# One product in eight left out of a last quarter, norm factors moved behind sums, softmax by heads

## The chip, the cores and the metric

The kernel runs on one core of one Trainium2 chip. Its time is the device time of an execution in microseconds (us); of several runs the median is taken. One further execution was recorded by the hardware profiler, and all rows in the profile's views are of that one.

## What is computed

A trunk of two layers over 16 + 512 = 528 positions of width 1024, in float32. Each layer is a mixer, a residual, an MLP and a residual; cut to what matters here:

```python
def sq_relu_mlp(h, norm_g, w_up, w_down):
    return jnp.square(jax.nn.relu(rms_norm(h, norm_g) @ w_up)) @ w_down   # 1024 -> 4096 -> 1024

h = h + even_mixer(h, ...)             # layer 0: attention (8 heads, window 128, sinks) beside a state-space scan
h = h + sq_relu_mlp(h, mlp_norm[0], w_up[0], w_down[0])
h = h + conformer_conv_module(h, ...)  # layer 1: pointwise, gate, causal depthwise convolution with 31 taps, layer norm, pointwise
h = h + sq_relu_mlp(h, mlp_norm[1], w_up[1], w_down[1])
return h[:, 16:]
```

`rms_norm` divides each position by its root mean square. This factor is one number r per position, so relu(r x) = r relu(x), and the square carries r squared, which may be multiplied behind the down projection.

## The kernel before

**Dense products.** Activations lie transposed: features on the 128 partitions, in 8 tiles, positions along the free axis. The positions are two streams, A with 272 (the 16 meta tokens and blocks 1 and 2) and B with 256 (blocks 3 and 4); in the second layer's MLP both have 256. Weights and activations are split into a high part of a float32 type that TensorE takes in one pass and a low part (the rest). A product of two tiles is three matmuls, high x high, high x low, low x high (`products`, L456). `dense` (L468) runs over output tiles n and the k-tiles of the inner dimension; a result gathers in a PSUM bank and is handed to an evacuation thread. The weight split is made on the chip, for each stream again: `th_load` fetches a piece (tile name `wr`) of 8 k-tiles (pool `wp`) or 4 (pool `wm`), `th_cast` makes the high part `wh` on ScalarE (L280), `th_low` the low part `wl` on VectorE (L254) or GpSimd (L256).

**An MLP** (`mlp`, L1317) goes by quarters q of the 4096 inner features: 8 output tiles of the up projection, then 8 of the down projection with those as inner k-tiles, one stream at a time. A stage's name gives its kind, layer, quarter and stream: `up13B` is the up projection of layer 1, quarter 3, stream B. The up evacuation (`ev_up`) takes relu times the norm's factor `rb` on VectorE, the square and the high part `ah` on ScalarE, the low part `al` on VectorE. In quarter 0 the factor isn't known yet: there relu stands alone, and the down evacuation multiplies by the factor's square. `add_h` adds each quarter's result to the residual `h`; `fin` (L1604) adds the last one and sends it out.

**Order of the work.** `main` (L1381) goes: first projection `in` for both streams; output projection `out` of A; quarters 0 and 1 of A's first MLP, beside which attention and scan of blocks 3 and 4 run on; `out` of B; quarters 2 and 3 of A; first pointwise product `pw` of A; the four quarters of B; `pw` of B; second pointwise product of A; four quarters of A's second MLP (`up10A` to `dn13A`); second pointwise product of B; four quarters of B (`up10B` to `dn13B`). The depthwise convolutions (`th_conv`, L1484) run on VectorE beside the MLPs: stream A's beside the first MLP of B, stream B's beside the second MLP of A; layer norms (`th_ln`) follow them. `wp` takes over the attention's memory, when the last attention block and the scan's norm of B are done.

**Who sets the order on the engines.** The kernel is written as threads; a planner (`Sched`, L66) emits their operations one at a time, by a cost table. An operation can have several ways (VectorE or GpSimd); `emit` takes the one that ends first by the plan, plus a handicap that the way may carry (`bias`: 3000 ns against VectorE for low parts while the convolutions run, 0 in the last stages). Among threads the one that can start first goes, then the lower rank: evacuations 0.5, loads 0, casts 1, low parts 1 or 4, convolution 3, attention blocks 1 and 2 by `rank` 0.6, later ones 2. The plan counts a port that VectorE (with both inputs in SBUF) and GpSimd share.

**Attention** (`att(c)`, L883) for block c: for each of four head pairs the scores on TensorE (`att_a`), then on VectorE the bias and the row maximum (L907). `softmax(g)` starts when all four heads of a group have their maxima: a small operation on the maxima `am`, four exponentials on ScalarE with row sums, the sink's term `ae`, the reciprocal, scaling; then transposes (`att_b`) and the products with the values (`att_c`). `ssd_norm` (L1104) gates the scan's output with silu and normalises it for `out`, in units of blocks whose ranks `UR` gives.

## Time and profile before

| | before |
|---|---|
| time, median of 3 runs | 1241.56 us (1237.67 to 1242.43) |
| time of the profiled execution | 1237.84 us |
| its span, first to last instruction | 1236.1 us |
| granted TensorE clock, mean | 0.994 |
| busy: TensorE, VectorE, ScalarE, GpSimd | 1219.7, 861.5, 683.4, 549.5 us |
| moved from and to HBM | 190.62 MB read, 2.10 MB written |

How the views are read: PE is TensorE's matmul, PEld its weight load, DVE VectorE, ACT ScalarE, POOL GpSimd, SP the queue that issues DMAs. A row of the views by line gives source line, engine, operation, `out<-in` by tile names, shape, count, then busy time, mean duration in ns, and the idle time before these instructions with what ended it. A row of the timeline gives start, duration, engine, line, operation; in brackets the idle time before it. A row of busy time by stretch gives the stretch, its length, for PE, PEld, DVE, ACT and POOL the busy time and number of instructions, then the clock, the DMA share and GB/s. A row of the chain gives start, duration and what ran in the chain of work that ended last. Matmuls overlap, so a single one shows some 280 ns where the next one starts after less than half of it.

### The profile page before, as it was taken

The numbers are of one execution on the slowest core, as the hardware profiler recorded it, in microseconds if no ns is written. First come the engines' busy times: TensorE is split into PE (matmuls) and PEld (weight loads), VectorE is DVE, ScalarE is ACT, GpSimd is POOL, SyncE is SP. The second block draws the span as 40 slices with busy tenths as digits, with TensorE's granted clock in tenths as the row PEclk, the third lists the DMA queues.
The fourth block names the chain that finished last, engine by engine and source line by source line (L and its number), as shares of the span: only waits on it lengthen the run. The fifth ranks groups of instructions, "written<-read, shape, count | busy, mean of one in ns | idle before, by whom it ended". The sixth has DMA issues, their size and how long they took to land.

```text
span 1236.1 us, 25626 instructions
## 1 busy us (share of the span) xinstructions
PE 1219.7 (99%) x9939; PEld 1176.1 (95%) x9939; DVE 861.5 (70%) x1915; ACT 683.4 (55%) x1277; POOL 549.5 (44%) x339
## 2 busy tenths in 40 slices
PE   8999998999999999999999999999999999999998
PEld 7999887799898999999999999999999999999998
DVE  6745685787785675658989965589898626766664
ACT  6654235677475663654544568556345645644542
POOL 0112331354541111148888878888888781000000
PEclk8999999999999999999999999999999999999999
DMA  6323112344344765546555555565555566566562
GB/s 191 105 81 86 44 44 56 104 141 144 114 142 135 245 198 176 172 135 199 183 184 181 185 166 180 187 192 175 181 186 183 176 194 202 188 179 196 177 196 91
DMA packets 79961, 194.38 MB, mean 157 GB/s; under 512 B 8912, under 2 KB 16608, under 8 KB 79840
## 3 DMA queue, kind: packets, MB, share of 16 engines
q1 hardware_dynamic: 79840, 192.75, 50.2%
q8 instruction: 78, 1.28, 0.4%
q14 instruction: 43, 0.35, 0.1%
HBM read 190.62 MB, written 2.10 MB: 156 GB/s over the span
## 4 chain that ended last, share of the span: by engine, by line
PE 92%; DVE 3%; ACT 3%; issue 1%; DMA 1%; SPq 0%; DVEq 0%; ACTq 0%
PE in L308 11%; PE pw L308 9%; PE out L308 5%; PE dn00A L308 2%; PE up00A L308 2%; PE up01A L308 2%; PE up03A L308 2%; PE dn02A L308 2%; PE dn12A L308 2%; PE up03B L308 2%; PE dn13B L308 2%; PE dn12B L308 2%; PE dn11B L308 2%; PE dn10B L308 2%; PE dn11A L308 2%; PE dn03B L308 2%
## 5 line engine op out<-in xcount | busy, mean ns | idle before, releaser
L256 POOL TENSOR_TENSOR wl<-wr,wh 128x1024 fp32r<-128x1024 f32 (+1 forms) x292 | 519.2, 1798 | 432.1 <-ACT wh L280 315.3
L280 ACT CAST wh<-wr 128x512 fp32r<-128x512 f32 (+1 forms) x494 | 384.6, 801 | 287.7 <-PE in L308 35.1
L254 DVE TENSOR_TENSOR wl<-wr,wh 128x512 fp32r<-128x512 f32 (+1 forms) x202 | 189.3, 949 | 90.0 <-ACT wh L280 87.1
L261 DVE SCALAR_TENSOR_TENSOR conv<-U,vec,conv 128x256 f32<-128x256 f32 x464 | 211.3, 484 | 5.2
L308 PE MATMUL in<-xh,wh 128*128 128x272 f32 (+1 forms) x384 | 103.6, 296 | 1.4 <-ACT wh L280 1.2
L308 PE MATMUL in<-xl,wh 128*128 128x272 f32 (+1 forms) x384 | 100.8, 289 | 1.1 <-DVE xl L261 1.1
L308 PE MATMUL pw<-nh,wh 128*128 128x256 f32 (+1 forms) x320 | 80.3, 285 | 0.0
L308 PE MATMUL pw<-nl,wh 128*128 128x256 f32 (+1 forms) x320 | 80.1, 284 | 0.0
L308 PEld LDWEIGHTS in<-xh,wh 128*128 128x128 f32 x384 | 73.3, 191 | 6.9 <-issue 3.2
L308 PEld LDWEIGHTS in<-xl,wh 128*128 128x128 f32 x384 | 73.3, 191 | 2.3 <-DVE xl L261 2.0
L308 PE MATMUL in<-xh,wl 128*128 128x272 f32 (+1 forms) x384 | 66.9, 291 | 0.0
L308 PEld LDWEIGHTS pw<-nl,wh 128*128 128x128 f32 x320 | 60.3, 189 | 0.0
L308 PEld LDWEIGHTS pw<-nh,wh 128*128 128x128 f32 x320 | 60.2, 188 | 0.1
L308 PEld LDWEIGHTS in<-xh,wl 128*128 128x128 f32 x384 | 55.0, 192 | 1.6 <-issue 0.9
L308 PE MATMUL pw<-nh,wl 128*128 128x256 f32 (+1 forms) x320 | 48.4, 284 | 0.0
L276 ACT ACT_TABLE_LOAD x30 | 38.5, 1283 | 9.0 <-DMA hin<-in_h 4.6
L308 PEld LDWEIGHTS pw<-nh,wl 128*128 128x128 f32 x320 | 42.8, 188 | 0.0
L308 PE MATMUL out<-xh,wh 128*128 128x272 f32 (+1 forms) x128 | 33.0, 288 | 0.2 <-ACT acc L276 0.2
L308 PE MATMUL out<-xl,wh 128*128 128x272 f32 (+1 forms) x128 | 32.6, 285 | 0.0
L254 DVE TENSOR_TENSOR pw<-pw,rb 128x272 f32<-128x272 f32 (+1 forms) x32 | 14.1, 440 | 24.9 <-PE pw L308 24.9
L308 PEld LDWEIGHTS out<-xh,wh 128*128 128x128 f32 x128 | 24.1, 188 | 1.4 <-issue 0.8
L308 PEld LDWEIGHTS out<-xl,wh 128*128 128x128 f32 x128 | 24.1, 188 | 0.0
(597 smaller groups left out, 3642.5 us busy)
## 6 DMA issues: line engine op xcount, KB each, us to landing
wr<-in_w_up SPq DMA_DIRECT2D x84, 512.0 KB, 3.7
wr<-in_w_dn SPq DMA_DIRECT2D x84, 512.0 KB, 4.0
wr<-in_w_up SPq DMA_DIRECT2D x88, 256.0 KB, 4.3
wr<-in_w_dn SPq DMA_DIRECT2D x88, 256.0 KB, 4.3
wr<-in_w_p SPq DMA_DIRECT2D x36, 512.0 KB, 3.9
wr<-in_w_in SPq DMA_DIRECT2D x48, 256.0 KB, 2.9
wr<-in_w_out SPq DMA_DIRECT2D x36, 256.0 KB, 2.8
wr<-in_w_p SPq DMA_DIRECT2D x24, 256.0 KB, 5.2
```

Source lines behind the costliest of these rows:

```text
L254: ways = [("V", 1.04 * n + 145, lambda: nc.vector.tensor_tensor(o, a, b, op=op), sb(a) and sb(b))]
L256: ways.append(("G", 2.17 * n + 170, lambda: nc.gpsimd.tensor_tensor(o, a, b, op=op), True))
L261: lambda: nc.vector.scalar_tensor_tensor(o, a, s, b, op0=op0, op1=op1), sb(a) and sb(b))],
L276: return Op([("A", ns, lambda: nc.scalar.activation(o, a, f, **kw), False)], aps(o, accum), aps(a, scale, bias), table=TABLE.get(f, 0))
L280: return Op([("A", 0.836 * cols(o) + 192, lambda: nc.scalar.copy(o, a), False)], [o], [a])
L308: nc.tensor.matmul(o, lhsT=l, rhs=r, start=st, stop=sp)
```

## The change

**The last quarter of the second MLP** is done for both streams together (`mlp` with `last`). Its up projection runs with one set of weight pieces for both streams, output tiles in the order 0, 4, 1, 5, ... . Its down projection is a product of 2 x 2 blocks: two output tiles n and n + 1, two halves of the 8 k-tiles, two streams as two column blocks. A scheme with seven products in place of eight (Strassen's, in Winograd's form) is used for four such pairs. The weight factors of four products are sums of weight pieces, made by the new thread `th_sum` (VectorE or GpSimd, handicap half of `bias`) before they are split; the activation factors T1 to T4 are sums of squares, made and split by `sums_of`. Stream B's squares of the first four tiles aren't split themselves. `seven` issues the products M1 to M7; `ev` forms the four results and adds them to `h` in two steps each (`fin_part`), which are then sent out from `h` itself. `bias` is 600 there, and up to seven PSUM banks may be used.

**Order.** Stream A's quarters 0 to 2 are followed at once by the second pointwise product of B, then B's quarters 0 to 2, then the joint quarter 3.

**Quarters summed first.** For stream B's first MLP (four quarters) and stream A's second one (three quarters), no quarter uses the norm's factor in its up evacuation: relu is an operation of its own on ScalarE, and the down results are summed in SBUF (`tot`; the first quarter is copied there by ScalarE). The last one multiplies the sum by the factor's square and goes on to the residual. Quarter 0 of the other MLPs has its relu on ScalarE too, and so has the convolution's first tap (L1499 before).

**Softmax head by head.** Each head has a thread of its own, from its maximum to its exponential with row sum; `softmax` goes on when four heads are done.

**Planner.** `ssd_norm`'s ranks go from 1.5 to 0.5 and from 0.4 to 0.3. While an operation of rank 0.5 or lower that can use VectorE's SBUF port waits, GpSimd may not take a less urgent operation that would end after that one's start. `row_norm` uses one PSUM bank in place of two in turn.

```diff
+        rank = lambda th: th[1]() if callable(th[1]) else th[1]
+
+        urgent = min((max(th[3].dep, self.free["V"]) for th in self.threads if th[3] is not None and rank(th) <= URGENT
+                      and any(w[0] == "V" and w[3] for w in th[3].ways)), default=None)
         for th in self.threads:
             op = th[3]
             if op is None:
                 continue
-            t = min(self.start(op, w)[0] for w in op.ways)
+            ways = op.ways
+            if urgent is not None and rank(th) > URGENT:
+                ways = [w for w in ways if not (w[0] == "G" and w[3] and self.start(op, w)[1] > urgent)]
+                if not ways:
+                    continue
+            t = min(self.start(op, w)[0] for w in ways)
...
+    def expect_seven(pairs):
+
+
+        for one, two in pairs:
+            i = len(plan)
+            half = lambda j, x: (j, 4 * x)
+            plan.extend((("wp", one, 8, None), ("wp", two, 8, "raw"),
+                         ("wm", (ALU.add, half(i + 1, 0), half(i + 1, 1)), 4, "sum"),
+                         ("wm", (ALU.subtract, half(i, 0), half(i + 1, 0)), 4, "sum"),
+                         ("wm", (ALU.subtract, half(i + 2, 0), half(i, 0)), 4, "sum"),
+                         ("wm", (ALU.subtract, half(i, 1), half(i + 4, 0)), 4, "sum"),
+                         ("wm", half(i + 1, 1), 4, "half")))
+            uses.extend((4, 4, 2, 1, 2, 1, 1))
...
+    def th_sum():
+        i = 0
+        while True:
+            yield lambda: i < len(plan) or over
+            if i >= len(plan):
+                return
+            if plan[i][3] == "sum":
+                op, (a, x), (b, y) = plan[i][1]
+                yield lambda: a in raws and b in raws
+                t = yield take(wm, [128, 4, 128], F32, "raw", 4, "ws")
+                o = TT(t, raws[a][:, x:x + 4], raws[b][:, y:y + 4], op, True)
+                o.ways[0] += (bias[0] / 2,)
+                yield o
+                raws[i] = t
+                used_raw(a, b)
+            i += 1
...
+        heads_done = [set(), set()]
+
+        def head(g, i):
+            mi = m[g][:, i:i + 1]
+            yield STT(mi, mi, -1.0, nsink[:, 4 * g + i:4 * g + i + 1], ALU.mult, ALU.min)
+            yield ACT(Sx[g][:, i, :nk], Sx[g][:, i, :nk], AF.Exp, bias=mi, accum=d[g][:, i:i + 1])
+            heads_done[g].add(i)
...
+                spawn(head(g, i), rank(c, 0.6), "att")
         pm = mt.tile([128, 8, 16], F32, tag="pm", bufs=1, name=nm("pm"))
 
         def softmax(g):
-            sk = nsink[:, 4 * g:4 * g + 4]
-            yield STT(m[g], m[g], -1.0, sk, ALU.mult, ALU.min)
-            yield TT(e[g], m[g], sk, ALU.subtract)
-            for i in range(4):
-                yield ACT(Sx[g][:, i, :nk], Sx[g][:, i, :nk], AF.Exp, bias=m[g][:, i:i + 1], accum=d[g][:, i:i + 1])
+            yield lambda: len(heads_done[g]) == 4
+            yield TT(e[g], m[g], nsink[:, 4 * g:4 * g + 4], ALU.subtract)
...
-    UR = lambda u: {0: 1.5, 2: 0.4}.get(u[0], 1)
+    UR = lambda u: {0: 0.5, 2: 0.3}.get(u[0], 1)
...
+            j = n - first
             u = p[:, :w]
-            if q:
+            if late:
+                yield ACT(u, u, AF.Relu)
+            else:
                 yield after(key)
                 yield STT(u, u, 0.0, rb[s][:, :w], ALU.max, ALU.mult)
-            else:
-                yield TS(u, u, 0.0, None, ALU.max)
+            if last:
+                raw[s, j] = yield take(pool7[0], [128, 272], F32, "sq", 8)
+                r = raw[s, j][:, :w]
+                yield ACT(r, u, AF.Square)
+                drop(p)
+                sums.add((s, j))
+                if s == 0 or j >= 4:
+                    yield CP(ah[:, j, :w], r)
+                    yield TT(al[:, j, :w], r, ah[:, j, :w].bitcast(F32), ALU.subtract)
+                    up[i].add(j)
+                return
...
+            if late:
+
+                if tot is not None and late != "last":
+                    if late == "first":
+                        tot[n] = yield take(pool7[0], [128, 272], F32, "sq", 8)
+                        yield CP(tot[n][:, :w], p[:, :w])
+                    else:
+                        yield TT(tot[n][:, :w], tot[n][:, :w], p[:, :w], ALU.add)
+                    drop(p)
+                    return
+                r2 = (acc if layer or tot is None else rb)[s][:, :w]
                 yield after(key)
-                if (key, 2) not in done:
+                if (key, 1) not in done:
+                    done.add((key, 1))
+                    yield TT(r2, rb[s][:, :w], rb[s][:, :w], ALU.mult)
                     done.add((key, 2))
-                    yield TT(r2, rb[s][:, :w], rb[s][:, :w], ALU.mult)
+                yield after((key, 2))
+                if tot is not None:
+                    yield TT(p[:, :w], tot[n][:, :w], p[:, :w], ALU.add)
+                    drop(tot.pop(n))
...
+    SEVEN = (0, 4, 1, 5, 2, 6, 3, 7)
...
+    def sums_of(k, w, there, raw, up, summed):
+        yield lambda: {(0, k), (1, k)} <= there
+        x1, y1 = raw[0, k], raw[1, k]
+        yield lambda: k in up[0]
+        yield TT(x1[:, :256], y1[:, :256], x1[:, :256], ALU.subtract, True)
+        yield lambda: (1, k + 4) in there
+        y2 = raw[1, k + 4]
+        yield TT(y1[:, :256], y2[:, :256], y1[:, :256], ALU.subtract, True)
+        yield lambda: k + 4 in up[1]
+        yield TT(y2[:, :256], y2[:, :256], x1[:, :256], ALU.subtract, True)
+        if w > 256:
+            yield VCP(y2[:, 256:w], x1[:, 256:w])
+        yield lambda: k + 4 in up[0]
+        x2 = raw[0, k + 4]
+        yield TT(x2[:, :w], y2[:, :w], x2[:, :w], ALU.subtract, True)
+        for i, t in ((1, x1), (3, y1), (2, y2), (4, x2)):
+            n = w if i in (2, 4) else 256
+            hi, lo = slot(i, 0, k, n), slot(i, 1, k, n)
+            yield CP(hi, t[:, :n])
+            yield TT(lo, t[:, :n], hi.bitcast(F32), ALU.subtract, True)
+            drop(t)
+            summed[i - 1].add(k)
...
+        def product(p, hi, lo, x, first, last_, ks=range(4)):
+            xh_, xl_, when, n = ops[x]
+            for k in ks:
+                yield lambda: when(k)
+                yield MM([(p[:, :n], hi[:, k], xh_(k), first and k == 0, False),
+                          (p[:, :n], hi[:, k], xl_(k), False, False)])
+            for k in ks:
+                yield MM([(p[:, :n], lo[:, k], xh_(k), False, last_ and k == 3)])
...
+            yield CP(m1[:, :w], b[0][:, :w])
...
+            yield TT(u[:, :w], m1[:, :w], b[3][:, :w], ALU.add)
...
+            yield TT(u7[:, :256], u[:, :256], b[2][:, 0:256], ALU.add)
...
+            yield TT(u[:, :256], u[:, :256], b[1][:, 0:256], ALU.add)
...
+            def p11():
+                yield from part(n, ca, w, m1[:, :w], lambda: b[0][:, :w], ALU.add, lambda: "M2" in at)
...
+            def p22():
+                yield from part(n + 1, cb, 256, u7[:, :256], lambda: b[1][:, 0:256], ALU.add, lambda: "M5" in at)
...
+            def p12():
+                yield from part(n, cb, 256, u[:, :256], lambda: b[1][:, 256:512], ALU.add, lambda: "M3" in at)
...
+            def p21():
+                yield from part(n + 1, ca, w, u7[:, :w], lambda: b[4][:, :w], ALU.subtract, lambda: "M4" in at)
...
+            terms = [("X1", "M1", x)]
+            for t, m in ((1, "M5"), (3, "M7"), (2, "M6")):
+                terms.append((f"T{t}", m, None))
+
+            for ks in ((0, 1, 2), (3,)) if n == 0 else (range(4),):
+                for i, (t, m, pc) in enumerate(terms):
+                    if pc is None:
+                        b.append((yield sbank))
+                        pc = yield from piece()
+                        terms[i] = (t, m, pc)
+                    yield from product(b[i], pc[0], pc[1], t, True, True, ks)
+                    if ks[-1] == 3:
+                        if i:
+                            done_with(*pc[:2])
+                        at.add(m)
+            yield lambda: "m1" in at
+            yield from product(b[0], x[0][:, 4:], x[1][:, 4:], "X2", True, True)
+            done_with(*x[:2])
+            at.add("M2")
+            pc = yield from piece()
+            yield from product(b[1][:, 256:], pc[0], pc[1], "Y2", True, True)
+            done_with(*pc[:2])
+            at.add("M3")
+            b.append((yield sbank))
+            pc = yield from piece()
+            yield from product(b[4], pc[0], pc[1], "T4", True, True)
+            done_with(*pc[:2])
+            at.add("M4")
...
                         if j == 0:
-                            yield TS(o, u, V("dww", k * TAPS), V("dwb", k), ALU.mult, ALU.add)
+                            yield ACT(o, u, AF.Identity, scale=V("dww", k * TAPS), bias=V("dwb", k))
...
-        for q in range(NQ):
-            yield from mlp(0, q, [(*A[1], *AH[1], add_h if q < NQ - 1 else prc[1])], 0, 0, 2)
+        tot = {}
+        for q, when in enumerate(("first", "next", "next", "last")):
+            yield from mlp(0, q, [(*A[1], *AH[1], prc[1])], 0, 0, 2, late=when, tot=tot)
...
-        def fin(n, c0, w, p):
-            o = yield take(lt[0], [128, 272], F32, "ut", 2)
-            yield TT(o[:, :w], p[:, :w], h[0][:, n, c0:c0 + w], ALU.add)
-            drop(p)
-            yield DMA(out[n * 128:n * 128 + 128, c0 - NM:c0 - NM + w], o[:, :w], 128)
-            drop(o)
-        for q in range(4):
-            yield from mlp(1, q, [(*F[0], *AH[0], add_h if q < 3 else fin)], 2 if q == 0 else 0, 6, 2)
+        def fin_part(n, c0, w, x, y, op, when):
+            hn = h[0][:, n, c0:c0 + w]
+            yield TT(hn, hn, x, ALU.add, True)
+            yield when
+            yield TT(hn, hn, y(), op)
+            yield DMA(out[n * 128:n * 128 + 128, c0 - NM:c0 - NM + w], hn, 128)
+        for q, when in enumerate(("first", "next", "last")):
+            yield from mlp(1, q, [(*F[0], *AH[0], add_h)], 2 if q == 0 else 0, 6, 2, late=when, tot=tot)
         yield from pause("ln")
+        drop(U, Y)
         bias[0] = 0.0
         yield from pw2(1, *AH[1], prf[1])
-        for q in range(4):
-            yield from mlp(1, q, [(*F[1], *AH[1], add_h if q < 3 else fin)], 2 if q == 0 else 0, 6, 2)
+        for q in range(3):
+            yield from mlp(1, q, [(*F[1], *AH[1], add_h)], 2 if q == 0 else 0, 6, 2)
+        wide[0] = 2
+        bias[0] = 600.0
+        yield from mlp(1, 3, [(*F[0], *AH[0], None), (*F[1], *AH[1], None)], last=fin_part)
```

More of the change, by code (lines that the diff above doesn't have):

```diff
@@ L53 @@
 SEM = 70.0
+URGENT = 0.5
 LATE = 600.0
@@ L1349, in ev_dn @@
                 yield TT(p[:, :w], p[:, :w], r2, ALU.mult)
             yield from post(n, c0, w, p)
[L1351 to L1354 removed]
+        nts = [first + j for j in (SEVEN if last else range(m))]
```

201 lines of the change are left out of this document (146 added, 55 removed).

## The prediction

> **What bounds the kernel now.** I read the page's busy times first, then the busy time by stretch, then the chain in order of time.
>
> ```profile
> span 1236.1 us, 25626 instructions
> PE 1219.7 (99%) x9939; PEld 1176.1 (95%) x9939; DVE 861.5 (70%) x1915; ACT 683.4 (55%) x1277; POOL 549.5 (44%) x339
> 583.00:606.00 23.00, 23.00 (x196) 23.00 (x195) 20.63 (x51) 13.73 (x25) 19.52 (x11) 1.00 0.59 179
> 1187.20:1210.00 22.80, 22.80 (x195) 22.80 (x195) 15.21 (x25) 13.32 (x25) 0.00 (x0) 1.00 0.58 183
> 1210.00:1236.00 26.00, 22.83 (x193) 22.63 (x192) 9.98 (x16) 5.18 (x8) 0.00 (x0) 0.99 0.25 81
> 1187.41 22.68 PE up13B L308 x192
> 1210.10 22.75 PE dn13B L308 x192
> ```
>
> TensorE is busy in 99% of the span, and from about 434 us on it does nothing but dense products: 192 matmuls of a quarter take 22.7 us without a hole, at full clock (1.00 in the clock column). One matmul of 128x256 costs 22.75 / 192 = 0.1185 us. VectorE with 20.63 of 23.00 us in the first MLP is loaded but hidden. So three things can move the time: the number of matmuls; the few holes in TensorE's work; and new waits where the other engines no longer keep up. All that only lightens VectorE where TensorE has no hole is worth nothing.
>
> **Part 1, seven products for eight.** Before, the last quarter's down projection was done stream by stream, 192 + 192 = 384 matmuls. Now four pairs of output tiles take 7 products x 4 k-tiles x 3 passes = 84 each, 336 in all. The up projection keeps its 384. So 48 fewer, 48 x 0.1185 = 5.7 us off the path. The price lies on the other engines:
>
> ```profile
> L254 DVE TENSOR_TENSOR wl<-wr,wh 128x1024 fp32r<-128x1024 f32 x22 | 27.0, 1225 | 20.5 <-ACT wh L280 20.5
> L254 DVE TENSOR_TENSOR wl<-wr,wh 128x512 fp32r<-128x512 f32 x14 | 9.0, 683 | 0.0
> L261 DVE SCALAR_TENSOR_TENSOR up13B<-up13B,rb 128x256 f32<-128x256 f32 x8 | 3.4, 427 | 0.0
> L254 DVE TENSOR_TENSOR al<-up13B,ah 128x256 fp32r<-128x256 f32 x8 | 3.4, 421 | 3.0 <-ACT ah L280 3.0
> L280 ACT CAST wh<-wr 128x512 fp32r<-128x512 f32 x14 | 8.0, 615 | 0.0
> L280 ACT CAST ah<-up13B 128x256 fp32r<-128x256 f32 x8 | 3.0, 374 | 0.3
> L276 ACT ACTIVATE up13B<-up13B 128x256 f32<-128x256 f32 x8 | 3.0, 371 | 7.4 <-DVE up13B L261 7.4
> L256 POOL TENSOR_TENSOR wl<-wr,wh 128x1024 fp32r<-128x1024 f32 x126 | 301.8, 2406 | 90.9 <-ACT wh L280 85.6 <-PE dn12A L308 2.9 <-PE dn10A L308 2.4
> L256 POOL TENSOR_TENSOR wl<-wr,wh 128x512 fp32r<-128x512 f32 x166 | 219.6, 1336 | 341.2 <-ACT wh L280 229.6 <-DVE wl L254 37.6 <-PE out L308 29.0
> L254 DVE TENSOR_TENSOR wl<-wr,wh 128x512 fp32r<-128x512 f32 x118 | 87.5, 753 | 22.3 <-ACT wh L280 20.0 <-PE out L308 1.9
> ```
>
> Per pair, in 84 x 0.1185 = 9.95 us of TensorE: the low parts of one 8-tile and five 4-tile pieces, 1.225 + 5 x 0.683 = 4.64 us of VectorE; four weight sums of 4 tiles, 4 x 0.683 = 2.73; seven additions with an operand in PSUM and four between SBUF tiles, 11 x 0.42 = 4.62. All of it on VectorE is 12.0 us, 2.05 more than TensorE takes. Lows, sums and the four SBUF additions may also go to GpSimd, which did nothing in this stretch before. It takes 1.336 for a 4-tile piece where VectorE takes 0.683. Moving two such pieces per pair is enough to bring VectorE below 10.7 and three below 9.95. The first pair's weights are prepared during the joint up projection, where one weight piece now serves 48 matmuls instead of 24. A later piece gets its buffer at the latest four products (4 x 12 x 0.1185 = 5.7 us) before TensorE reads it, and needs about 1.3 us (cast 0.615, low part 0.683), so some 4.4 us of lateness are absorbed. Without any help of GpSimd the shortage is 3 x 2.05 = 6.2, less 4.4, so 1.8 us of waiting; I take 0.5, since GpSimd is free, and keep 0 to 8 as bounds (8 is 4 x 2.05, nothing absorbed).
>
> The turn from up to down is new too. TensorE ends with k-tile 7 of stream B; from there run relu 0.43, square 0.37, three subtractions and a low part in turn (4 x 0.42) and two casts (2 x 0.37), about 3.2 us with the semaphores' steps. What covers it are the products of k-tiles 0 to 2 of the first four factors, 36 x 0.1185 = 4.3 us. A low part of 1.2 us queued ahead on VectorE would use that cover up: 0.7 us taken, between 0 and 3. The last quarter's own output additions and DMAs come pair by pair, and the final one is again one addition and one DMA, so the tail is costed at nothing. Part 1 in all: -5.7 + 0.5 + 0.7 = -4.5 us.
>
> The Trainium skill speaks against this part (SBUF — State Buffer, "Who interferes with whom"): a VectorE instruction with two SBUF inputs and a GpSimd one that reads SBUF exclude each other for a whole instruction. This trace leans that way: the same 4-tile low part takes 0.683 with GpSimd idle and 0.753 on the mean of all. What such a lock would make of the time is the last rival.
>
> **Part 2, softmax head by head.** A hole of TensorE stands where the second block's attention ends the first projection:
>
> ```profile
> 196.23 0.44 DVE L907 CUSTOM_DVE_ANT_0 S<-att_a,at 128x272 f32<-128x272 f32 x1 [2.02 <-PE att_a L308]
> 206.18 0.44 DVE L907 CUSTOM_DVE_ANT_0 S<-att_a,at 128x272 f32<-128x272 f32 x1
> 206.54 0.28 DVE L261 SCALAR_TENSOR_TENSOR am<-am,nsink 128x4 f32<-128x4 f32 x2
> 207.27 0.62 ACT L280 CAST wh<-wr 128x512 fp32r<-128x512 f32 x1 [5.53 <-PE in L308]
> 207.80 0.52 ACT L276 ACTIVATE S<-S,am 128x272 f32<-128x272 f32 x1
> 211.85 0.28 ACT L276 ACTIVATE ae<-ae 128x4 f32<-128x4 f32 x2
> 208.44 0.62 PE L308 MATMUL in<-xh,wl 128*128 128x256 f32 x4
> 213.42 0.47 PE L315 MATMUL att_b<-cm,pm 128*128 128x128 f32 x1 [4.36 <-DVE pm L254]
> 216.24 1.28 ACT L276 ACT_TABLE_LOAD   x1
> 217.54 1.11 ACT L276 ACTIVATE sz<-sz 128x1088 f32<-128x1088 f32 x1
> ```
>
> The heads' maxima come between 196.2 and 206.6, but the eight exponentials wait for the last maximum and run in one row from 207.80 to 211.85, while ScalarE had sat idle for 5.53 us just before. TensorE then waits 4.36 us. Head by head, six exponentials fit into that idle time; two are left after 206.6, at 0.5 us each, so they end near 207.9 instead of 211.85: 3.9 us earlier, and the wait shrinks from 4.36 to about 0.4. What is late next: stream A's early output projection starts sooner, and behind it the gated norm, whose silu waits in ScalarE's queue behind the exponentials (table load at 216.24, silu at 217.54). With the exponentials gone from 208 on, it can move up by the same 4 us or more, and the ranks of the norm's units are lowered to help it. I take the 3.9; the bounds are 0 (the norm stays where it is) and 7 (the two following waits for copies shrink too).
>
> The fourth block's softmax has the same form later on:
>
> ```profile
> 344.81 0.42 DVE L907 CUSTOM_DVE_ANT_0 S<-att_a,at 128x272 f32<-128x272 f32 x1
> 356.43 0.22 DVE L261 SCALAR_TENSOR_TENSOR am<-am,nsink 128x4 f32<-128x4 f32 x2
> 376.79 2.38 DVE L254 TENSOR_TENSOR xl<-xc,xh 128x512 fp32r<-128x512 f32 x2
> 377.39 0.51 ACT L276 ACTIVATE S<-S,am 128x272 f32<-128x272 f32 x1
> 393.56 2.11 PE att_c L308 x12
> 395.74 3.67 DMA wr<-in_w_out
> 399.49 1.05 ACT wh L280
> 398.01 0.66 PE L308 MATMUL dn01A<-xh,wl 128*128 128x272 f32 x4
> 400.58 0.38 PE L308 MATMUL out<-oh,wh 128*128 128x256 f32 x1 [1.91 <-ACT wh L280]
> ```
>
> Its last maximum is there at 345.2, its last exponential runs at 377.4. The attention ends with att_c at 395.67, and only then is its memory given to the large weight buffers, whose first load (3.67) and cast TensorE awaits for 1.91 us at 400.58. Exponentials that start with each head end some 15 to 25 us earlier; then the stream's norm (its last low parts end at 379.2) sets the release, 16 us ahead of 395.7, and the 1.91 us go. I take -1.9, between -1.9 and 0.
>
> **Part 3, norm's factor last, relu on ScalarE, first tap on ScalarE.** Each quarter of stream B's first and stream A's second MLP then needs no factor before its square. A relu costs 0.43 on VectorE now and some 0.37 on ScalarE by the square's row; sums replace additions one for one, with two more per tile in the last of them. All of it lies beside the dense products. It matters only through the convolution, because the kernel now goes to the second half's pointwise product 45 us sooner: stream A's last quarter is taken out from between.
>
> ```profile
> L268 DVE TENSOR_SCALAR conv<-U,vec 128x256 f32<-128x256 f32 x16 | 8.5, 544 | 0.3
> L261 DVE SCALAR_TENSOR_TENSOR Y<-U,vec,conv x16: 471/474/478, 636.2 to 956.0; 128x256 f32<-128x256 f32 x16
> 981.03 22.68 PE up13A L308 x192
> 988.40 0.42 DVE L254 TENSOR_TENSOR al<-lnq,ah 128x256 fp32r<-128x256 f32 x1 [0.91 <-ACT ah L280]
> ```
>
> The second convolution ends at 956.0 and its layer norm at 988.8; the pointwise product would now begin where up13A begins, 981.0. Its eighth k-tile is read 14 x 0.1185 = 1.7 us later, at 982.7: 6.1 us too soon. But VectorE is the convolution's limit, and it loses 24 relus x 0.427, 16 operations x 0.42 in the first quarter's output and 8 taps x 0.544 = 21 us ahead of 956. So the layer norm ends near 970 and 0 is my value for the wait, 6.1 the other bound. The small waits for norm factors in the middle may shrink: -0.3.
>
> **The sum** is -4.5 - 3.9 - 1.9 - 0.3 = -10.6 us. Against the profiled execution (1237.84) that is 1227.2. The median of the three timed runs, 1241.56, lies 3.7 higher, which would give 1231.0. I name 1229.0. About 0.5%, 6.2 us, is what a measurement here can tell from no change.
>
> **Rivals.**
> 1. The exponentials' gain is taken back by the next wait (the gated norm, or extra table loads at 1.28 us each when exponentials fall between silus and square roots): -10.6 + 3.9, 1231.1. For it: the silu and the norm follow closely. Against it: ScalarE's idle 5.53 us. The Trainium skill (ScalarE: Activation LUTs, "Rules for kernel authors") holds with it: do all functions of one table set before the next. By that rule three switches would cost the whole 3.9.
> 2. The last quarter is bound by VectorE: the 8 us bound instead of 0.5, 1234.7.
> 3. The layer norm is late at the pointwise product: + 6.1, 1233.3.
> 4. The new ranks and the rule on GpSimd reorder the first 430 us, and the 5.8 us that attention gains are lost in other holes, or a few more: 1233 to 1238, no change that can be told.
> 5. Slower: the split work of the last quarter goes to GpSimd and VectorE's SBUF operations stand behind it. A pair then needs 2.406 + 9 x 1.336 + 4 x 0.42 = 16.1 us against 9.95, over four pairs + 24.7 in place of the 0.5: 1251.4. It decides from about 12.9 us a pair, where 4 x 2.9 eats all gains. For it: in the stretches with GpSimd's help nearly all lows went there (19.52 of 23.00 us). Against it: the bias towards GpSimd is 3000 there and only 600 here, and the planner counts the shared port.
>
> **How the numbers follow.** My forecast 0.52; rival 1 0.14, 2 0.10, 3 0.05, 4 0.11, 5 0.08. Faster by over 0.5%: the forecast, most of rival 1, and that part of 2, 3 and 4 in which only half the price falls due: 0.67. Within 0.5%: 0.24. Slower: 0.09. The range goes from 1220 (7 in place of 3.9, and no waits in the last quarter: 1237.84 - 5.7 - 7 - 1.9 - 0.3 = 1222.9, less half the runs' scatter) to 1240, which takes in rivals 1 to 4 on the median's side and leaves out 5.
>
> **What would show it.** Right: 336 matmuls of the last down projection in about 41 us, with little idle time of TensorE before them; att_b of the second block within 1 us of the last `in` matmul; no hole at the start of the second output projection; the pointwise product right behind dn12A. Wrong: TensorE waiting for `wl` or the new sums in the last 45 us; low parts of 1.3 us piling up on GpSimd there; more table loads than now and a hole before the output projection of stream A; waits for `ah` or `al` of the layer norm.

## Result and the profile after

| | before | after |
|---|---|---|
| time, median | 1239.93 us (1237.67 to 1242.43, 4 runs) | 1230.39 us (1230.29 to 1231.28, 4 runs) |
| ratio to before | | 0.9924 (95% interval 0.9901 to 0.9948) |
| profiled execution, its span | 1237.84, 1236.1 us | 1230.29, 1228.5 us |

The change makes the kernel 0.8% faster; the named time was 1229.0. The 1241.56 us that the prediction started from was the median of three of these four runs of the kernel before. In the kernel after, the helpers' lines have moved: L308 became L317 (matmul), L254 L263, L261 L270, L276 L285, L280 L289, L256 L265.

The page of the kernel after, and its busy time by stretch (columns as before):

```profile
span 1228.5 us, 25576 instructions
PE 1213.2 (99%) x9891; PEld 1169.4 (95%) x9891; DVE 869.2 (71%) x1921; ACT 714.7 (58%) x1391; POOL 532.5 (43%) x335
583.00:606.00 23.00, 23.00 (x197) 23.00 (x197) 21.16 (x51) 15.40 (x31) 19.74 (x11) 1.00 0.61 185
975.45:998.20 22.75, 22.75 (x194) 22.75 (x193) 17.08 (x30) 13.44 (x28) 0.06 (x1) 1.00 0.58 180
1137.24:1182.60 45.36, 45.36 (x387) 45.36 (x386) 32.61 (x60) 21.17 (x49) 10.43 (x9) 1.00 0.23 70
1182.60:1225.16 42.56, 40.95 (x337) 39.98 (x336) 37.19 (x72) 15.84 (x30) 13.16 (x10) 1.00 0.30 90
```

TensorE's work has shrunk by 6.5 us, the span by 7.6. The second pointwise product of B (fourth row) runs without a hole. The joint up projection (fifth row) has no idle time, but the joint down projection (last row) takes 42.56 us for 336 matmuls, while TensorE is busy in 40.95 of them only. The chain of waits shows where it is torn:

```profile
1137.40 45.35 PE up13AB L317 x384
1182.76 5.70 PE dn13AB L317 x48
1189.94 10.82 PE dn13AB L317 x88
1201.26 10.67 PE dn13AB L317 x88
1212.43 9.88 PE dn13AB L317 x80
1222.81 2.64 PE dn13AB L317 x20
```

There are four breaks, one per pair of output tiles (the first a short one, the other three 0.51 us of waiting each), and none at the turn from up to down. The timeline around the second break, of TensorE, VectorE and GpSimd:

```profile
1198.55 1.74 POOL L265 TENSOR_TENSOR ws<-wr,wr 128x512 f32<-128x512 f32 x1 [7.17 <-DVE wl L263]
1200.25 1.27 POOL L265 TENSOR_TENSOR wl<-ws,wh 128x512 fp32r<-128x512 f32 x1
1200.79 0.42 DVE L263 TENSOR_TENSOR sq<-sq,dn13AB 128x256 f32<-128x256 f32 x1 [0.90 <-PE dn13AB L317]
1201.12 2.78 DVE L263 TENSOR_TENSOR h<-h,sq 128x256 f32<-128x256 f32 x4
1201.26 0.39 PE L317 MATMUL dn13AB<-ah,wh 128*128 128x256 f32 x1 [0.51 <-DVE sq L263]
1201.48 1.47 POOL L265 TENSOR_TENSOR ws<-ws,wr 128x512 f32<-128x512 f32 x1
```

Two things are to be seen. First, VectorE's addition of M5 waited for TensorE, and TensorE then waits for that addition in the middle of M3: M3 gathers in the second half of M5's bank, and here the kernel's semaphores let reading one half and writing the other only take turns. Second, the four additions `h<-h,sq` of 256 columns take 2.78 us, though one costs 0.42 in the prediction's rows: two of them stand while GpSimd's operations at 1200.25 and 1201.48 run. One took 1.51 us, from 1201.72 to 1203.23, and ended 0.28 us after the second of these.

At the two holes of before, and at what came behind them:

```profile
205.47 0.51 ACT L285 ACTIVATE S<-S,am 128x272 f32<-128x272 f32 x1
205.98 0.29 ACT L285 ACTIVATE ae<-ae 128x4 f32<-128x4 f32 x2
209.16 0.27 PE L324 MATMUL att_b<-cm,pm 128*128 128x128 f32 x1
238.04 0.39 PE L317 MATMUL out<-oh,wh 128*128 128x272 f32 x1 [1.70 <-ACT h L289]
241.31 0.39 PE L317 MATMUL out<-xh,wh 128*128 128x272 f32 x1 [0.52 <-ACT h L289]
395.91 0.28 PE L317 MATMUL out<-oh,wh 128*128 128x256 f32 x1
969.73 0.42 DVE L263 TENSOR_TENSOR al<-lnq,ah 128x256 fp32r<-128x256 f32 x1 [0.29 <-ACT ah L289]
```

The second block's last exponential is done at 206.0, and `att_b` at 209.16 has no wait in brackets (4.36 before). The second output projection begins at 395.91 without one too (1.91 before). New are two waits at 238.04 and 241.31, 2.2 us together, for ScalarE's copies of `h`. Exponentials stand ahead of the first of these copies on ScalarE:

```profile
236.60 0.52 ACT L285 ACTIVATE S<-S,am 128x272 f32<-128x272 f32 x1
237.12 0.51 ACT L285 ACTIVATE S<-S,am 128x272 f32<-128x272 f32 x1
237.63 0.36 ACT L289 COPY h<-out 128x272 f32<-128x272 f32 x1
```

The layer norm's last low part ends at 970.15, 5.3 us before the pointwise product.

### The profile page after: what moved, and what is told of

It is laid out like the page before. It is cut to its first block, busy times and chain, and to the rows that moved or that the text cites. A ratio compares the mean times of both kernels' runs of the same rounds, so it can differ in the third digit from the quotient of the medians.

```text
span 1228.5 us, 25576 instructions
## 1 busy us (share of the span) xinstructions
PE 1213.2 (99%) x9891; PEld 1169.4 (95%) x9891; DVE 869.2 (71%) x1921; ACT 714.7 (58%) x1391; POOL 532.5 (43%) x335
## 4 chain that ended last, share of the span: by engine, by line
PE 93%; ACT 3%; DVE 3%; issue 1%; DMA 0%; SPq 0%; DVEq 0%; ACTq 0%
PE in L317 12%; PE pw L317 9%; PE out L317 6%; PE up13AB L317 4%; PE dn13AB L317 3%; PE dn00A L317 2%; PE up01A L317 2%; PE up02A L317 2%; PE dn01A L317 2%; PE up00A L317 2%; PE up03A L317 2%; PE dn02A L317 2%; PE dn02B L317 2%; PE up10A L317 2%; PE up12A L317 2%; PE dn12B L317 2%
## 5 line engine op out<-in xcount | busy, mean ns | idle before, releaser
L265 POOL TENSOR_TENSOR wl<-wr,wh 128x512 fp32r<-128x512 f32 x275 | 486.8, 1788 | 579.4 <-ACT wh L289 501.2
L289 ACT CAST wh<-wr 128x512 fp32r<-128x512 f32 (+1 forms) x472 | 367.6, 797 | 244.4 <-issue 27.5
L263 DVE TENSOR_TENSOR wl<-wr,wh 128x512 fp32r<-128x512 f32 (+1 forms) x197 | 183.8, 943 | 94.7 <-ACT wh L289 92.6
L270 DVE SCALAR_TENSOR_TENSOR conv<-U,vec,conv 128x256 f32<-128x256 f32 x464 | 209.2, 486 | 9.6 <-ACT conv L285 2.7
L317 PE MATMUL in<-xh,wh 128*128 128x272 f32 (+1 forms) x384 | 104.0, 297 | 1.5 <-ACT wh L289 1.5
L317 PE MATMUL in<-xl,wh 128*128 128x272 f32 (+1 forms) x384 | 100.9, 289 | 1.3 <-DVE xl L270 1.3
L317 PE MATMUL pw<-nh,wh 128*128 128x256 f32 (+1 forms) x320 | 80.7, 286 | 0.1
L317 PE MATMUL pw<-nl,wh 128*128 128x256 f32 (+1 forms) x320 | 80.2, 284 | 0.0
L317 PEld LDWEIGHTS in<-xh,wh 128*128 128x128 f32 x384 | 73.4, 191 | 6.8 <-issue 3.4
L317 PEld LDWEIGHTS in<-xl,wh 128*128 128x128 f32 x384 | 73.5, 191 | 2.5 <-DVE xl L270 2.1
L317 PE MATMUL in<-xh,wl 128*128 128x272 f32 (+1 forms) x384 | 66.5, 291 | 0.0
L317 PEld LDWEIGHTS pw<-nh,wh 128*128 128x128 f32 x320 | 60.2, 188 | 0.5 <-ACT sqh L285 0.3
L317 PEld LDWEIGHTS pw<-nl,wh 128*128 128x128 f32 x320 | 60.3, 189 | 0.0
L317 PEld LDWEIGHTS in<-xh,wl 128*128 128x128 f32 x384 | 54.8, 192 | 1.5 <-issue 0.7
L317 PE MATMUL pw<-nh,wl 128*128 128x256 f32 (+1 forms) x320 | 48.1, 284 | 0.0
L317 PEld LDWEIGHTS pw<-nh,wl 128*128 128x128 f32 x320 | 42.7, 188 | 0.0
L317 PE MATMUL out<-xh,wh 128*128 128x272 f32 (+1 forms) x128 | 33.3, 289 | 0.5 <-ACT h L289 0.5
L317 PE MATMUL out<-xl,wh 128*128 128x272 f32 (+1 forms) x128 | 32.7, 284 | 0.0
L263 DVE TENSOR_TENSOR pw<-pw,rb 128x272 f32<-128x272 f32 (+1 forms) x32 | 14.0, 439 | 26.0 <-PE pw L317 25.7
L317 PE MATMUL up13AB<-nl,wh 128*128 128x256 f32 x128 | 31.1, 281 | 0.0
L317 PE MATMUL up13AB<-nh,wh 128*128 128x256 f32 x128 | 31.1, 281 | 0.0
```

The source lines that it names most:

```text
L263: ways = [("V", 1.04 * n + 145, lambda: nc.vector.tensor_tensor(o, a, b, op=op), sb(a) and sb(b))]
L265: ways.append(("G", 2.17 * n + 170, lambda: nc.gpsimd.tensor_tensor(o, a, b, op=op), True))
L270: lambda: nc.vector.scalar_tensor_tensor(o, a, s, b, op0=op0, op1=op1), sb(a) and sb(b))],
L289: return Op([("A", 0.836 * cols(o) + 192, lambda: nc.scalar.copy(o, a), False)], [o], [a])
L317: nc.tensor.matmul(o, lhsT=l, rhs=r, start=st, stop=sp)
```

## Experiments

The theory at the start was the prediction's: each part acts where it was said to; what is missing of the sum sits in the last quarter and behind the exponentials. The rivals were its own: VectorE too busy in the last quarter, GpSimd in its way, the layer norm late, and the planner's new order. Of each run the median and the ratio to the kernel before on the same chip are given (before there: 1237.29 for the first four, 1238.17 and 1238.54 for the next two groups).

**Heads alone**, on the kernel before:

```diff
...
+                spawn(head(g, i), rank(c, 0.6), "att")
...
-            for i in range(4):
-                yield ACT(Sx[g][:, i, :nk], Sx[g][:, i, :nk], AF.Exp, bias=m[g][:, i:i + 1], accum=d[g][:, i:i + 1])
+            yield lambda: len(heads_done[g]) == 4
```

> The kernel before with softmax head by head and nothing else. Theory: the attention part of the gain comes from this edit alone. The wait of 4.36 us ahead of the second block's transposes goes, so does the 1.91 us at the second output projection; up to 2.2 us may come back as waits for the copies of h. 3 to 6 us faster than before (ratio 0.995 to 0.9975). Rival, that the lowered ranks and the rule on GpSimd made this gain: within 1 us of before, and the 4.36 us wait stands as it was.

Measured: 1235.71 us, ratio 0.9985 (0.9975 to 0.9996), a gain of 1.6 us by the medians where 3 to 6 were expected. TensorE's waits in its timeline:

```profile
211.70 1.08 PE L308 MATMUL att_c<-pt,vtok 128*64 128x512 f32 x4 [1.39 <-ACT pt L280]
445.23 0.59 PE L308 MATMUL up02A<-nh,wh 128*128 128x272 f32 x1 [2.35 <-DVE al L254]
```

The holes of 4.36 and 1.91 are gone here too, so the heads alone remove both. Behind the first one a wait of 1.39 for `pt` has come up, the copies of `h` stop TensorE at 238 and 241 us as in the kernel after, and a new hole of 2.35 stands in the third quarter of A's first MLP. In the profile this quarter begins 4.6 us earlier than before, and its down projection only 1.2 us earlier: the hole, with 3.4 us at half clock behind it, took the rest.

**Planner alone**, on the kernel before:

```diff
+URGENT = 0.5
...
-    UR = lambda u: {0: 1.5, 2: 0.4}.get(u[0], 1)
+    UR = lambda u: {0: 0.5, 2: 0.3}.get(u[0], 1)
```

with the rule in the planner's choice.

> The kernel before with the lowered ranks of the gated norm and the rule that keeps GpSimd from late work, nothing else. Theory: these only reorder work beside TensorE's; within 1.5 us of before. Rival, that they made the gain of the first 400 us: 4 to 5 us faster, with the 4.36 us wait shorter.

Measured: 1244.87 us, ratio 1.0069 (1.005 to 1.0087): slower, which neither the theory nor the rival had. The first hole stays, and the second one grows from 1.91 to 4.82, which is 2.9 of the 6.3 us that this run has lost in its profile by the start of A's third quarter:

```profile
405.61 0.45 PE L317 MATMUL out<-oh,wh 128*128 128x256 f32 x1 [4.82 <-ACT wh L289]
```

**Eight products** in the joint last quarter:

```diff
...
-        yield from mlp(1, 3, [(*F[0], *AH[0], None), (*F[1], *AH[1], None)], last=fin_part)
+        yield from mlp(1, 3, [(*F[0], *AH[0], fin8), (*F[1], *AH[1], fin8)], 0, 6, 2)
```

(`fin8` adds a result to `h` and sends it out.)

> The changed kernel with the joint last quarter kept (one set of weight pieces for both streams) but eight products in its down projection, 384 matmuls. Theory: 48 matmuls more cost 5.7 us, and the 2.9 us of waits that the changed kernel has in its last down projection go: 2.5 to 3 us slower than the changed kernel, no wait of TensorE in the last 90 us. Rival, that the seven products give back all they save: within 0.5 us of the changed kernel. Rival, that the waits come from the joint quarter itself and not from the scheme: 5.7 us slower, with the waits still there.

Measured: 1233.07 us, ratio 0.997 (0.9958 to 0.9982), 2.7 us over the kernel after by the medians. The two were not timed side by side, and by their ratios the distance is larger, 0.9970 against 0.9924 and, measured again below, 0.9934; the stage itself is the closer measure:

```profile
1186.35:1231.70 45.35, 45.35 (x385) 45.35 (x384) 13.12 (x22) 5.25 (x8) 1.82 (x1) 1.00 0.17 56
```

So 384 matmuls take 45.35 us without a wait, and seven products save 45.35 - 42.56 = 2.8 us of the possible 5.7. The rivals, nothing saved or waits that come from the joint quarter itself, fall.

**Factors early**: part 3 undone.

```diff
-            yield from mlp(0, q, [(*A[1], *AH[1], prc[1])], 0, 0, 2, late=when, tot=tot)
+            yield from mlp(0, q, [(*A[1], *AH[1], add_h if q < 3 else prc[1])], 0, 0, 2)
...
-                yield ACT(u, u, AF.Relu)
+                yield TS(u, u, 0.0, None, ALU.max)
```

and the same for A's second MLP and the first tap.

> The changed kernel with norm's factors back in each quarter's up evacuation, relu and the convolution's first tap back on VectorE. Theory, by the prediction's third part: VectorE loses its 21 us of relief, the second convolution and its layer norm end some 20 us later than the 928.8 and 970.1 of the changed kernel, so at 985 to 990, and the pointwise product that wants it at 975.5 waits 4 to 7 us in all: 4 to 7 us slower than the changed kernel. Rival, that this relief is worth nothing: within 1 us.

Measured: 1240.2 us, ratio 1.0026 (1.0014 to 1.0038), some 10 us over the kernel after by the medians where 4 to 7 were expected (8.3 by the spans of the two profiles). The pointwise product of B, in the stretches view and the timeline:

```profile
979.04:1006.76 27.72, 26.12 (x194) 24.54 (x193) 17.57 (x35) 17.26 (x38) 5.97 (x4) 0.94 0.51 162
980.57 0.39 PE L317 MATMUL pw<-ah,wh 128*128 128x256 f32 x1 [0.65 <-ACT ah L289]
982.27 0.38 PE L317 MATMUL pw<-ah,wh 128*128 128x256 f32 x1 [0.38 <-ACT ah L289]
```

It takes 27.72 us instead of 22.75: the layer norm is late by the mechanism of the third rival, which part 3 keeps away. Only 1.6 of these 5.0 us are idle time; the mean clock of 0.94 comes from 3.4 us at half clock from 984 us on. Most of the rest of the difference is a hole of 2.4 us at 445 us, as in the run with heads alone.

**The kernel after again**, the mark for the next runs.

> The changed kernel itself, unaltered, as the mark for the three others on the same chip. All theories: ratio to the kernel before 0.990 to 0.995, near 1230.4 us.

Measured: 1230.15 us, ratio 0.9934 (0.9919 to 0.9948).

**A bank of its own for M3:**

```diff
+            b.append((yield sbank))
...
-            yield from product(b[1][:, 256:], pc[0], pc[1], "Y2", True, True)
+            yield from product(b[4], pc[0], pc[1], "Y2", True, True)
...
```

> The changed kernel with one edit: the product M3 gathers in a PSUM bank of its own, not in the second half of M5's bank. Theory (one bank shared by M5's half, which VectorE still reads, and M3's half, which TensorE writes, makes the two engines wait in turn): the four waits of about 0.7 us in the joint down projection go, the stage takes 39.8 to 40.5 us instead of 42.56, the whole 2 to 3 us less than the changed kernel. Rival (VectorE has too much to do there, as the prediction's second rival had it): the same waits come back at the next bank, the stage stays within 0.5 us of 42.56. A second rival: six banks a pair are too many, the next pair's first product waits for one; then the stage is longer than 42.56.

Measured: 1230.28 us, ratio 0.9939 (0.9923 to 0.9955). The stage takes 42.04 us: 0.5 less, not 2 to 3, and the whole is the same. The waits within M3 are gone, and the next product that needs a bank waits in their place:

```profile
1195.90:1206.40 10.50, 10.50 (x90) 10.44 (x89) 10.40 (x15) 3.09 (x5) 4.24 (x3) 1.00 0.49 151
1207.91 1.19 PE L317 MATMUL dn13AB<-Y,wh 128*128 128x256 f32 x8 [0.64 <-DVE h L263]
```

VectorE is busy for 10.40 of 10.50 us in one pair. So the shared bank is where the delay shows, and VectorE's lateness stands behind it; the theory that the bank alone does it fell. The second rival's wait is seen too (one for a bank), but the stage is not longer.

**Rank of the early copies:**

```diff
-            spawn(begin(n, p), 3, f"out{s}ev")
+            spawn(begin(n, p), 1, f"out{s}ev")
```

> The changed kernel with one edit: the thread that copies stream A's early output projection out of PSUM has rank 1 instead of 3, ahead of the third block's head-by-head exponentials (rank 2). Theory (the head-by-head exponentials, queued on ScalarE ahead of these copies, make TensorE wait 1.70 + 0.52 us at 238 to 241 us): these waits go, stage checkpoints from the first MLP on come about 2 us earlier. Rival (the copies wait for something else): no change at 238 to 241. The new rank also lets the planner order the first 430 us anew, so the holes after 250 us can move; a total between -3 and +3 us is compatible with the theory, the trace at 238 us decides.

Measured: 1229.13 us, ratio 0.9922 (0.9907 to 0.9938). The view of waits shows none of TensorE between 225 and 246 us, against 2.2 us for `h` in the kernel after. From the start of A's output projection to the start of its third quarter 210.33 us pass instead of 211.98; a wait of 0.64 us within the third quarter takes part of it back. The theory holds; the gain in the whole is too small for the interval. The last stage, which this edit does not touch, took 43.0 us here, and 42.6 in the kernel after again, with factors early and with the old planner: a single profile's difference of 0.5 us there says little.

**Both edits together.**

> The two edits together. If both theories hold and nothing else moves: 4 to 5 us less than the changed kernel, near 1226 us, ratio to the kernel before 0.988 to 0.991. If the own bank alone helps: 2 to 3 us less.

Measured: 1227.7 us, ratio 0.9917 (0.99 to 0.9934); the stage takes 41.77 us. By the medians that is 2.4 us less than the kernel after, not 4 to 5, and the intervals overlap: the own bank again brings less than its theory had.

**Weights of the last quarter on VectorE only:**

```diff
-        bias[0] = 600.0
+        bias[0] = -100000.0
```

> The changed kernel with one edit: in the joint last quarter the weights' low parts and sums stay on VectorE (the handicap against VectorE is set far below zero); only additions to h and squares may still go to GpSimd. Theory (a VectorE operation on SBUF alone stands still while a GpSimd one runs, so GpSimd's help gives back about what it takes): the joint down projection stays within 1 us of 42.56, VectorE's additions of 256 columns go back to about 0.42 us each from 0.78 on the mean. Rival (the two work side by side, and the seven operations of about 0.69 us that come back to VectorE are missing): the stage takes 45 to 47 us. The prediction's own step without GpSimd had 1.8 us of waiting, so 41.6 us.

Measured: 1229.3 us, ratio 0.9918 (0.9903 to 0.9933). The whole differs from the kernel after by less than the intervals can tell, but the stage became shorter, 41.32 us, though VectorE took seven operations of 0.69 us back and gave three of 0.42 to GpSimd. (The mean of 0.78 us in the expectation is that of the run with the own bank; in the kernel after it is 0.693.) The stretch, and the groups of VectorE, first in the kernel after, then here:

```profile
L263 DVE TENSOR_TENSOR h<-h,sq 128x256 f32<-128x256 f32 x13 | 8.3, 693 | 0.0
L263 DVE TENSOR_TENSOR wl<-ws,wh 128x512 fp32r<-128x512 f32 x10 | 7.7, 790 | 0.1
L263 DVE TENSOR_TENSOR h<-h,dn13AB 128x256 f32<-128x256 f32 x15 | 5.4, 410 | 0.4 <-PE dn13AB L317 0.4
```

```profile
1183.49:1224.81 41.32, 40.49 (x337) 39.83 (x336) 35.90 (x76) 15.90 (x29) 6.76 (x6) 1.00 0.29 93
L263 DVE TENSOR_TENSOR wl<-ws,wh 128x512 fp32r<-128x512 f32 x12 | 8.1, 688 | 0.1
L263 DVE TENSOR_TENSOR h<-h,sq 128x256 f32<-128x256 f32 x11 | 4.0, 419 | 0.0
```

The additions fall from 693 to 419 ns, the low parts from 790 to 688: 13 x 0.274 + 10 x 0.102 = 4.6 us that VectorE had spent standing, against 7 x 0.69 = 4.8 us that GpSimd had taken off it. Additions with an operand in PSUM (410 ns) had not been slowed.

**More on GpSimd:**

```diff
-        bias[0] = 600.0
+        bias[0] = 3000.0
```

> The changed kernel with one edit: the handicap of the last quarter is 3000 ns, as beside the convolutions, so 28 more low parts and sums go to GpSimd. Theory (the two engines exclude each other on SBUF operations): GpSimd's 1.3 to 2.4 us pieces become the bound, the joint down projection takes 46 to 60 us instead of 42.56, the whole 3 to 17 us more than the changed kernel; this is the prediction's last rival with its condition met. Rival (work moved off VectorE lightens it): the stage takes 40 to 42 us.

Measured: 1247.8 us, ratio 1.0078 (1.0058 to 1.0099). The stage takes 59.85 us:

```profile
1182.31:1242.16 59.85, 46.63 (x337) 44.73 (x336) 36.61 (x54) 16.00 (x30) 44.90 (x32) 0.89 0.20 62
1199.79 0.58 PE L317 MATMUL dn13AB<-U,wh 128*128 128x256 f32 x1 [5.64 <-DVE U L263]
L263 DVE TENSOR_TENSOR h<-h,sq 128x256 f32<-128x256 f32 x16 | 20.3, 1329 | 0.0
L263 DVE TENSOR_TENSOR h<-h,dn13AB 128x256 f32<-128x256 f32 x15 | 5.4, 411 | 2.0 <-PE dn13AB L317 2.0
```

By the medians this is 17.6 us more than the kernel after. VectorE has 18 operations fewer than there, and is busy for about as long (36.61 us, 37.19 there): an addition of SBUF tiles now takes 1329 ns, one with PSUM still 411. Part of the stage's length is the clock, 0.89 on the mean (last section).

**All three edits**: own bank, rank 1, weights on VectorE.

> The changed kernel with three edits: M3's own bank, rank 1 for the early copies, and the weights' low parts and sums of the last quarter on VectorE. Theory (what keeps the joint down projection 2 to 3 us above its matmuls is VectorE standing behind GpSimd): the stage takes 40.5 to 42 us, the whole 2 to 5 us less than the changed kernel. Rival (VectorE simply has too much work there): 43 to 46 us.

Measured: 1225.98 us, ratio 0.9894 (0.9876 to 0.9912). The stage is down to its matmuls:

```profile
1181.39:1221.07 39.68, 39.68 (x338) 39.64 (x336) 36.19 (x76) 15.78 (x29) 6.95 (x6) 1.00 0.31 98
```

336 matmuls in 39.68 us, no idle time, below the range of the expectation, with VectorE as busy as in the run with the weights on VectorE alone. This is the fastest version: by the medians 4.2 us under the kernel after, with an interval below the one of the kernel after's second measurement (0.9919 to 0.9948), though not wholly below that of the first (0.9901 to 0.9948).

**Old planner**, in the kernel after: ranks and rule undone.

```diff
-URGENT = 0.5
+URGENT = -1.0
```

and `UR` as before.

> The changed kernel with the planner's part undone: the gated norm's units at their old ranks, and no rule that holds GpSimd back. Alone, that part made the kernel before 8.5 us slower. Theory 1 (it pays only together with the head-by-head softmax and the relu on ScalarE, and is about neutral or useful there): undone, the kernel takes 0 to 4 us more, with a hole near 445 us as in the run with heads only. Theory 2 (it costs here too, hidden behind the other gains): undone, the kernel takes 3 to 8 us less.

Measured: 1231.49 us, ratio 0.9941 (0.9924 to 0.9958). No difference to the kernel after that the intervals can tell; the hole expected at 445 us did not come, one of 1.28 us for a weight copy came at 291 us instead. What cost 8.5 us alone is neutral beside the other parts: theory 1, at its weak end.

## Why the prediction was right, and where it was not

That the named 1229.0 lies within 1.4 us of the measured 1230.39 is partly luck. The sum of the prediction is 3.0 us too large against the profiles (table below), the named time was taken between two bases, 1227.2 and 1231.0, and the later groups have the kernel before at 1237.29 to 1238.54 us. Measured again, the gain is 0.66%. The direction came as forecast and both holes closed; the last quarter's share, and what came up behind the first hole, did not.

Stage by stage from the two profiles (a stage is measured from one first matmul to the next):

| term | predicted | measured |
|---|---|---|
| first hole, up to A's output projection | -3.9 | -5.1 |
| from there to A's third quarter (hole at the second output projection) | -1.9 | 0.0 |
| from there to the end of the last `dn12A` | -0.3 | -0.3 |
| pointwise product of B | 0 | -0.2 |
| B's quarters 0 to 2 | 0 | +1.0 |
| last quarter, both streams (90.73 to 87.92) | -4.5 | -2.8 |
| tail | 0 | -0.2 |
| sum | -10.6 | -7.6 |

**Part 1, the count of matmuls: right.** The run with eight products and the last version differ by 45.35 - 39.68 = 5.7 us in that stage, which is the 48 x 0.1185 of the prediction.

**Part 1, "I take 0.5, since GpSimd is free": this step failed**; the stage lost 2.9 us. Being idle did not make GpSimd's help free. The prediction's bounds held (0 to 8). The sign that it named, TensorE waiting for `wl` or the new sums, did not show in the kernel after; the waits are for the additions that empty PSUM. Its 1.8 us without any help lie near the 41.32 - 39.68 = 1.6 measured with the weights on VectorE, but by chance: GpSimd still had six operations there, and with M3 in its own bank the same load on VectorE left no wait at all. The prediction weighed this lock as its last rival, but only at the price of a heavy bias; even at a bias of 600 it gave back 4.6 of the 4.8 us. The Trainium skill (SBUF — State Buffer, "Who interferes with whom") says that a VectorE instruction with two SBUF inputs and a GpSimd one that reads SBUF lock each other out for a whole instruction, and that one with at most one SBUF input, outside the two-port modes, is not touched. The runs agree with both halves: 693 and 1329 ns against 419, and 410 and 411 ns with an operand in PSUM. With the condition of that rival set up, the stage became 59.85 - 42.56 = 17.3 us longer; the 24.7 of the prediction had GpSimd at work all the time, and it was busy in 44.90 of the 59.85 us.

The second half of the loss is the bank that M5 and M3 share, which the prediction did not look at. Alone, an own bank brought 0.5 us and VectorE without GpSimd 1.2; with both (beside the new rank, which acts 940 us earlier and alone left the stage at 43.0) the stage lost all its 2.9 us of waits. A reading that fits is that each edit takes away one of two reasons for the same waits, so that they are worth more together; as the planner orders the stage anew with each edit, the 2.9 us cannot be split cleanly between them. The Trainium skill (PSUM — Partial Sum Buffer, "Summary: rules for kernel authors") tells to read PSUM beside a running matmul from another bank, and to guard by bank; the wait of 0.51 us at 1201.26 between two halves of one bank is what that guard costs here.

**Part 1, the turn: wrong, but by 0.7 us.** No wait stands there.

**Part 2, the first hole: right in mechanism, too small by 1.2.** `att_b` starts 4.26 us earlier with no wait left. The other 0.84 come from the clock: from `att_b` to A's output projection 9.50 us passed before and 8.66 after. The part up to the second run of `att_b`, at half clock before, shrank from 4.75 to 3.44 (last section), and a longer wait for `pt` (0.80 against 0.29) took 0.5 back.

**Part 2, "what is late next": wrong place.** The prediction looked at the gated norm. Late next were the copies of A's early output projection, behind the third block's exponentials in ScalarE's queue; with head-by-head threads these come up earlier, at a lower rank number than the copies. That has the form of the first rival, with 2.2 of its 3.9 us, but not its two causes: the gated norm did not stop TensorE there, and the table loads stayed at 30. The run with the other rank shows the cause. The hole of 1.91 went as predicted; the new one took the gain back.

**Part 3: right.** The layer norm ended at 970.15 ("near 970"), nothing waited. Undone, the product took 5.0 us more, near the bound of 6.1.

**Rival 4** holds for the planner alone (8.5 us lost by the ratio) and not in company. Why B's first quarter takes 1.0 us more (two waits for VectorE's `acc` at 1001 and 1004 us) was not tested.

## What to carry to other kernels

Price an idle GpSimd by what its operations hold up: where VectorE works on SBUF tiles at the same time, count the help of GpSimd as nothing until a trace shows otherwise. Before an output is packed into the free half of a PSUM bank, ask who still reads the other half. When an operation is split so that its parts start early, look in the same engine's queue for the small copies that a TensorE wait ends on.

## What the hardware showed beyond that

In these profiles TensorE's clock is halved around its longer holes, so a hole costs more than its length. Stretches of before, of the kernel after at the same place, and of the run with more on GpSimd (the clock is the third number from the end):

```profile
211.46:218.29 6.83, 4.87 (x14) 2.38 (x15) 2.42 (x11) 6.15 (x14) 0.00 (x0) 0.50 0.27 79
```

```profile
209.16:215.99 6.83, 5.96 (x28) 2.50 (x26) 2.55 (x5) 6.70 (x12) 0.30 (x1) 1.00 0.41 119
```

```profile
1197.98:1204.81 6.83, 5.02 (x23) 5.02 (x24) 2.18 (x6) 0.99 (x2) 2.75 (x3) 0.50 0.44 126
1215.05:1221.88 6.83, 5.29 (x25) 5.32 (x26) 2.06 (x5) 2.01 (x5) 4.49 (x5) 0.50 0.62 184
```

All five holes of 3.4 us or more behind the first 20 us (4.36 before, two of 4.7 and 4.8 with the planner alone, 5.64 and 3.5 with more on GpSimd) had 3.4 or 6.8 us at 0.50 that began in them or within 0.2 us behind. Holes of 1.7 to 2.4 us had 3.4 us of it in some profiles and none in others. Eight of the fourteen profiles show such a stretch near 123 us as well, where TensorE has no hole; its cause stays open, and with it part of the scatter of 2 to 3 us between runs of one kernel.
